# The last expert pairs of a decoder layer: where the combines of pairs 13 and 14 and the overflow branch stand

## Chip, cores and metric

One NeuronCore of a Trainium2 chip runs the whole layer in one launch. The metric is the device time of one execution in microseconds (us); lower is better.

## The reference, cut to what matters

The layer is a mixer of three branches (pooling, latent attention, attention into a memory), a residual add, then a mixture of experts with 32 experts of which each of the 512 tokens takes 2, another residual add and a last RMSNorm. Only the experts and the last norm are touched here. `D_MODEL` is 1024, `D_EXPERT` 256.

```
h2 = rms_norm(x, ffn_norm_g[l])
x = x + hierarchical_moe(h2, ...)
return rms_norm(x, final_norm_g)

def hierarchical_moe(h, ...):
    ...                                  # top group, top 2 experts of it, their weights
    def run_block(args):
        toks, e = args
        xb = x_pad[toks]
        a = jax.nn.silu(xb @ w_gate_e[e]) * (xb @ w_up_e[e])
        return a @ w_down_e[e]
    ...
    y = yb.reshape(R, D) * row_w[:, None].astype(yb.dtype)
    out = jax.ops.segment_sum(y, row_tok, num_segments=T + 1)[:T]
```

## The kernel before

The 32 experts are handled as 16 pairs, 64 token slots for each expert of a pair, so that a pair fills the 128 partitions. `W[e]` are the weights of an expert, in twelve pieces of 128x512; two pieces make one load of 512 KB. All loads go through one queue (SyncE, SP) into a ring of 36 places: tiles `e` of the pools W0 (tag `e0`, 6 places) and W1 (tag `e1`, 18 places), and tiles `r`, `wh`, `wl`, `m`, `ac` left from earlier stages. `used(n)` moves the ring on and lets further loads be written down.

The program is traced in the order in which the text calls the helpers (`tc.manual_schedule()`): each engine executes its own instructions in that order, and waits on semaphores where data come from another engine. For each pair `p` a list of short names gives the order:

- `U0` to `U7` (`up`, L1126): the gate and up products, step k of 8, accumulated in one bank `gu`. `U7` ends with silu on ScalarE (ACT, L1134) and a product on VectorE (DVE, L1135) into tile `a`.
- `t` (`turn`, L1137): TensorE transposes `a`, ACT copies it back (L1142).
- `D` (`down`, L1144, with `down_half`, L1161): the product with the down weights. Its two halves are scaled by the routing weight; ACT writes the rounded part (L1151), DVE the rest (L1152), into two tiles `y`. In step `p` these are called for pair `p-1`.
- `c` (`combine`, L1170): one of eight pieces of putting a pair's `y` onto its tokens. Two matmuls with the one-hot matrix `PT` put half a row tile in a bank (`xe` of two banks or `cb`, of which there is one), and DVE adds it to `ACC`, the residual stream in SBUF with tokens on partitions (L1176).
- `x0`, `x1` transpose the next pair's gathered tokens, `w` builds `PT`, `o`, `j`, `f` prepare a later pair (nothing, once there is none).

Pairs 0 to 8 add their output in DRAM by a scattering DMA. Pairs 9 to 14 are combined into `ACC`; the eight pieces wait in the list `todo` and are taken by the `c` of the order lists, four in a pair's own following step, four in the next. The last pair (15) isn't combined: TensorE gathers the `ACC` rows of its tokens into two banks (L1356, sixteen passes of 128x512 in the trace, four for each row tile), its down product is added there, and the rows get their own norm and go to the output by a scattering DMA (L1377). All 512 rows are normed and written before that (L1365, L1366); the scatter waits for these writes.

An expert with more than 64 tokens sets `flag`. `overflow()` then runs the pairs again for the rest. It stands in a branch (`tc.If`, L1295) that all engines read and jump over when `flag` is 0. In the profiled execution its body was jumped over. An engine that jumps adds to its own semaphores what the body would have added, after its own earlier work is done.

The lists of orders, and what is done ahead of the last pair:

```
SEQM = "o U0 c U1 j c U2 c t c U3 x0 D n U4 w c U5 c x1 c U6 f c U7".split()
SEQL = "t D U0 U1 U2 U3 U4 U5 U6 U7".split()
...
        if last:
            while todo:
                todo.pop(0)()
            ...
            with tc.If(nc.values_load(flag[0:1, 0:1], min_val=0, max_val=1) > 0):
```

Of the kernel before, what the change touches and what calls it, by code (L numbers as in the profile page):

```python
# [9 lines left out]
F32 = mybir.dt.float32  # L10
F32R = mybir.dt.float32r
BF16 = mybir.dt.bfloat16
I32 = mybir.dt.int32
AF = mybir.ActivationFunctionType
# [5 lines left out]
T = 512  # L20
D = 1024
# [20 lines left out]
def trunk_and_moe(ctx, tc, a, out):  # L42
    nc = tc.nc
    v, s, g, pe = nc.vector, nc.scalar, nc.gpsimd, nc.tensor
# [34 lines left out]
    def nm(b):  # L79
        n[0] += 1  # L80
        return f"{b}{n[0]}"
# [26 lines left out]
    def bank(p, tag, bufs, shape=(128, 512)):  # L108
        return p.tile(list(shape), F32, tag=tag, name=nm(tag), bufs=bufs)
# [9 lines left out]
    eps = cst.tile([128, 1], F32, name="eps")  # L119
# [99 lines left out]
    order = tc.manual_schedule()  # L219
# [104 lines left out]
    w = WS.use("w_in", 0)  # L324
# [172 lines left out]
    for h_ in range(XHEADS):  # L497
        fill()
        fill()
        w = WS.use("w_mk", h_)  # L500
# [3 lines left out]
        t = mt()  # L504
# [5 lines left out]
    for c in range(4):  # L510
        fill()
        fill()
        w = WS.use("w_mv", c)
# [19 lines left out]
    for h_ in range(XHEADS):  # L533
# [3 lines left out]
        for i in range(4):  # L537
            S = bank(PA, "s", 2)
# [18 lines left out]
        hs = slice(h_ * 128, (h_ + 1) * 128)  # L557
# [39 lines left out]
    b = swap(kr)  # L597
# [13 lines left out]
    scale = 192.0 ** -0.5  # L611
# [23 lines left out]
    for d in range(KD):  # L635
        w = WS.use("w_bpm", d)
# [15 lines left out]
    NP = NE // 2  # L652
# [147 lines left out]
    for h_ in range(HEADS):  # L800
        for op in SEQ:
# [22 lines left out]
            elif k == "V" and h_ % 2:  # L824
                p = (h_ + 1) // 2
# [44 lines left out]
    W1 = Scope("w1", side="right").p  # L870
# [55 lines left out]
    ACC = row_major()  # L926
# [65 lines left out]
    def ct2(dt=F32):  # L992
        return C2.tile([128, 1024], dt, tag="y", name=nm("y"), bufs=3)
# [58 lines left out]
    PC = Scope("pc", space=PSUM).p  # L1052
# [6 lines left out]
    extra = [False]  # L1059
# [4 lines left out]
    class Pair:  # L1064
# [78 lines left out]

        def down(self):  # L1144

            y = self.y = [ct2()] if self.scattered else [ct2(F32R), ct2(F32R)]
            for hf in range(2):
                hs = slice(hf * 512, (hf + 1) * 512)
                ps = self.down_half(hf)
                if not self.scattered:  # L1150
                    s.activation(y[0][:, hs], ps, AF.Copy, scale=self.wt)  # L1151
                    v.scalar_tensor_tensor(y[1][:, hs], ps, self.wt, y[0][:, hs].bitcast(F32), op0=OP.mult, op1=OP.subtract)  # L1152
                elif hf:
                    v.tensor_scalar(y[0][:, hs], ps, self.wt, None, op0=OP.mult)  # L1154
                else:
                    s.activation(y[0][:, hs], ps, AF.Copy, scale=self.wt)
            if self.scattered:
                g.indirect_dma_start(out=xo[:, :], out_offset=bass.IndirectOffsetOnAxis(ap=self.ix[:, :1], axis=0), in_=y[0], in_offset=None,  # L1158
                                     bounds_check=T - 1, oob_is_err=False, compute_op=OP.add)
# [113 lines left out]

    SEQ0 = "X0 b1 X1 b2 X2 U0 X3 U1 X4 U2 X5 U3 X6 U4 X7 U5 j0 o U6 j1 x0 U7 L x1 j2 j f".split()
    SEQM = "o U0 c U1 j c U2 c t c U3 x0 D n U4 w c U5 c x1 c U6 f c U7".split()
    SEQL = "t D U0 U1 U2 U3 U4 U5 U6 U7".split()
    todo = []
    fs = cst.tile([128, 5, 4], F32, name="fs")  # L1280

    def wide():
        return W0.tile([128, 2, T], F32, tag="e0", name=nm("e"), bufs=6).rearrange("p a b -> p (a b)")

    for p, q in enumerate(PP):
        q.wts = [W[2 * p], W[2 * p + 1]]
        last = p == NP - 1
        if p == NP - 2:
            gf = XG[0]
            g.dma_start(gf, a["final_g"].broadcast_to([128, D]))  # L1290
        if last:
            while todo:
                todo.pop(0)()
            order.__exit__(None, None, None)
            with tc.If(nc.values_load(flag[0:1, 0:1], min_val=0, max_val=1) > 0):  # L1295
                extra[0] = True
                overflow()
                extra[0] = False
            order = tc.manual_schedule()
            order.__enter__()  # L1300

            q.rw = fs[:, 0, 3:4]
            v.tensor_tensor(q.rw, q.rs, q.wt, op=OP.mult)
        for op in (SEQ0 if p == 0 else SEQL if last else SEQM):
            n_ = int(op[1]) if len(op) > 1 else p + 3
            if op[0] == "U":
                q.up(n_)
                if n_ % 2:
                    used(2)
            elif op == "c" and todo:  # L1310
                todo.pop(0)()
            elif op[0] == "X":
                q.pick_x(n_)
            elif op[0] == "b":
                PP[n_].fetch(PP[n_].by_slot(tokr, 2)[:, 0:1])
            elif op[0] == "x" and not last:
                PP[p + 1].turn_x(n_)
            elif op == "w" and SC <= p < NP - 1:
                q.where()
            elif op == "L":  # L1320
                PP[0].place(PP[0].it[:, 6:7])
                for i in range(RING - 4, RING):
                    load_piece(i)
            elif op == "n" and p == 1:
                tiles()
            elif op[0] in "ojf" and n_ < NP:
                if op[0] == "o":
                    PP[n_].onehot()
                if op[0] == "j":
                    PP[n_].info()  # L1330
                if op[0] == "f":
                    PP[n_].fetch(PP[n_].it[:, 6:7])
            elif op == "t":
                PP[p - 1].turn()
            elif op == "D":
                PP[p - 1].down()
                used(4)
                if p == SC:
                    ACC = row_major()
                    for t in range(4):  # L1340
                        g.dma_start(ACC[:, t].rearrange("p a b -> p (a b)"), xo[t * 128:(t + 1) * 128])
                if p > SC:
                    todo += [lambda i=i, q=PP[p - 1]: combine(i, q) for i in range(8)]

    junk, o = wide(), wide()
    hs = [slice(hf * 512, hf * 512 + 512) for hf in range(2)]
    s.activation(fs[:, 4, 0:1], q.a[:, 0:1], AF.Sqrt, scale=0.0)
    ys = [bank(PC, "y", 2) for hf in range(2)]
    for t in range(4):
        x = ACC[:, t].rearrange("p a b -> p (a b)")  # L1350
        todo.pop(0)()
        todo.pop(0)()
        if t == 1:
            q.turn()
        for hf in range(2):
            pe.matmul(ys[hf], lhsT=q.P[:, t].bitcast(F32), rhs=x[:, hs[hf]], start=t == 0, stop=False)  # L1356
        f = fs[:, t]
        s.activation(junk, x, AF.Square, accum_out=f[:, 0:1])
        s.activation(f[:, 1:2], f[:, 0:1], AF.Sqrt, bias=eps[:, 0:1], scale=1.0 / D)
    for hf in range(2):  # L1360
        q.down_half(hf, ys[hf])
    for t in range(4):
        x = ACC[:, t].rearrange("p a b -> p (a b)")
        v.reciprocal(fs[:, t, 2:3], fs[:, t, 1:2])  # L1364
        v.scalar_tensor_tensor(x, x, fs[:, t, 2:3], gf, op0=OP.mult, op1=OP.mult)  # L1365
        sync.dma_start(out[0, t * 128:(t + 1) * 128], x)  # L1366
    f = fs[:, 4]
# [103 lines left out]
```

## Time and profile before

| what | value |
| --- | --- |
| median of 3 runs | 805.36 us (804.89 to 809.42) |
| the profiled execution's own time | 807.81 us |
| its span in the profile | 806.0 us |
| TensorE (PE) busy | 779.0 us, 97% |
| DVE, ACT, GpSimd (POOL) busy | 365.8, 304.4, 276.8 us |
| mean granted TensorE clock | 0.991 of full speed |

The profiled execution is 1.8 us longer than its span, and 2.45 us longer than the median. A "busy" TensorE is not one at its peak, so its share says little; what counts near the end is which wait ends last. Times below are in us from the start of the span.

### The profile page before, as it was taken

The page shows a single profiled execution, that of the slowest core. Times are in us where ns is not written, and L with a number is a line of the kernel's source. Part 1 is how long each engine was busy: PE and PEld are TensorE (multiplying, and loading weights), DVE is VectorE, ACT ScalarE, POOL GpSimd, SP SyncE. Part 2 cuts the span into 40 slices and gives each one's busy share as a digit, 9 for nine tenths or more (in the row PEclk, how much of TensorE's full clock was granted, in tenths as well). Part 3 has the DMA queues.
Part 4 walks back from the last instruction along what each step waited for, and adds up shares of the span by engine and source line. Part 5 has one row for each costly group of instructions (what it writes and reads, how often), then busy time and mean ns, then how long its engine had stood idle before and what let it go on. Part 6 is the DMA issues. An engine that isn't in the chain of part 4 may idle for free. (4 is left out here: it accounts for less than half of the span.)

```text
span 806.0 us, 10157 instructions
## 1 busy us (share of the span) xinstructions
PE 779.0 (97%) x3741; PEld 524.1 (65%) x3743; DVE 365.8 (45%) x675; ACT 304.4 (38%) x626; POOL 276.8 (34%) x169
## 2 busy tenths in 40 slices
PE   7999999999999999999999999999999999999894
PEld 3778888888887888788888888754333333333331
DVE  5668693243455134677774532323121223454424
ACT  6254453343336444655553321213222222222232
POOL 3256677533332688422225644311121212000000
PEclk9999999999999999999999999999999999999988
DMA  6533333321121322111224489979999999999933
GB/s 223 179 105 105 105 105 136 125 105 71 62 92 38 98 95 92 46 47 56 79 87 176 147 313 340 372 257 354 394 370 397 391 374 392 405 354 408 405 125 120
DMA packets 53509, 164.17 MB, mean 204 GB/s; under 512 B 7906, under 2 KB 9058, under 8 KB 53456
## 3 DMA queue, kind: packets, MB, share of 16 engines
q1 hardware_dynamic: 46224, 149.14, 50.3%
q0 software_dynamic: 4640, 9.90, 3.8%
q10 hardware_dynamic: 2592, 4.46, 1.5%
q8 instruction: 30, 0.49, 0.2%
q14 instruction: 23, 0.19, 0.1%
HBM read 158.82 MB, written 11.53 MB: 211 GB/s over the span
## 5 line engine op out<-in xcount | busy, mean ns | idle before, releaser
L125 POOL TENSOR_TENSOR wl<-r,wh 128x1024 fp32r<-128x1024 f32 (+3 forms) x75 | 167.7, 2244 | 210.8 <-ACT wh L180 189.7
L180 ACT CAST wh<-r 128x1024 fp32r<-128x1024 f32 (+3 forms) x85 | 82.1, 972 | 32.0 <-PE mm L199 12.6
L1131 PE MATMUL gu<-e,u 128*64 128x512 f32 x336 | 88.8, 607 | 0.9 <-DMA e<-in_w_e 0.9
L198 PE MATMUL mm<-g,wh 128*128 128x512 f32 x180 | 71.9, 400 | 0.0
L199 PE MATMUL mm<-g,wh 128*128 128x512 f32 x180 | 70.2, 390 | 0.0
L1107 ACT ACTIVATE u<-xe,PR 128x128 f32<-128x128 f32 x120 | 34.2, 367 | 67.4 <-PE xe L1103 67.3
L471 PE MATMUL mm<-box,wh 128*128 128x512 f32 x144 | 56.8, 394 | 0.9 <-ACT wh L180 0.9
L472 PE MATMUL mm<-box,wh 128*128 128x512 f32 x144 | 56.3, 391 | 0.0
L201 PE MATMUL mm<-g,wl 128*128 128x512 f32 x180 | 52.7, 391 | 0.0
L1158 POOL DMA_INDIRECT xo<-y,ix x9 | 14.3, 1594 | 89.9 <-DVE ix L1082 79.7
L435 ACT ACTIVATE m<-s,st 128x256 f32<-128x256 f32 (+3 forms) x48 | 24.3, 508 | 54.4 <-DVE st L433 53.9
L1131 PEld LDWEIGHTS gu<-e,u 128*64 128x64 f32 x336 | 20.4, 135 | 33.0 <-issue 26.1
L1167 PE MATMUL y<-e,u 128*64 128x512 f32 x160 | 38.9, 600 | 0.4 <-DMA e<-in_w_e 0.4
L201 PEld LDWEIGHTS mm<-g,wl 128*128 128x128 f32 x180 | 33.8, 188 | 7.5 <-POOL wl L125 0.2
L198 PEld LDWEIGHTS mm<-g,wh 128*128 128x128 f32 x180 | 34.0, 189 | 6.5
L199 PEld LDWEIGHTS mm<-g,wh 128*128 128x128 f32 x180 | 33.9, 188 | 6.4
L476 PE MATMUL mm<-box,wl 128*128 128x512 f32 x144 | 36.6, 390 | 0.0
L198 PE MATMUL mm<-box,wh 128*128 128x512 f32 x78 | 31.7, 406 | 0.5 <-DVE g L283 0.5
L471 PEld LDWEIGHTS mm<-box,wh 128*128 128x128 f32 x144 | 27.1, 188 | 6.7 <-ACT wh L180 1.3
L1154 DVE TENSOR_SCALAR y<-y,it 128x512 f32<-128x512 f32 x9 | 6.8, 751 | 54.1 <-PE y L1167 54.1
L476 PEld LDWEIGHTS mm<-box,wl 128*128 128x128 f32 x144 | 27.0, 188 | 5.8
L472 PEld LDWEIGHTS mm<-box,wh 128*128 128x128 f32 x144 | 27.1, 188 | 5.3
(358 smaller groups left out, 1657.3 us busy)
## 6 DMA issues: line engine op xcount, KB each, us to landing
e<-in_w_e SPq DMA_DIRECT2D x124, 512.0 KB
r<-in_w_in SPq DMA_DIRECT2D x37, 512.0 KB
r<-in_w_e SPq DMA_DIRECT2D x15, 512.0 KB
wh<-in_w_e SPq DMA_DIRECT2D x15, 512.0 KB
wl<-in_w_e SPq DMA_DIRECT2D x15, 512.0 KB
m<-in_w_e SPq DMA_DIRECT2D x30, 256.0 KB
r<-in_w_bpm SPq DMA_DIRECT2D x8, 512.0 KB
r<-in_w_bl SPq DMA_DIRECT2D x8, 512.0 KB
```

Of the source, the lines that this page charges most:

```text
L125: eng.tensor_tensor(lo, x, hi.bitcast(F32), op=OP.subtract)
L180: s.copy(hi[:, :cols], r[:, :cols])
L198: pe.matmul(ps, lhsT=lh, rhs=rh, start=start and i == 0, stop=False)
L199: pe.matmul(ps, lhsT=lh, rhs=rl, start=False, stop=False)
L201: pe.matmul(ps, lhsT=ll, rhs=rh, start=False, stop=stop and i == m - 1)
L435: s.activation(P[:, :w], S[:, :w], AF.Exp, bias=st4[:, 0:1], accum_out=st4[:, 1:2])
L471: pe.matmul(ps, lhsT=lh, rhs=rh, start=k == 0, stop=False)
L472: pe.matmul(ps, lhsT=lh, rhs=rl, start=False, stop=False)
L476: pe.matmul(ps, lhsT=ll, rhs=rh, start=False, stop=k == KD - 1)
L1107: s.activation(x[:, j], ps[:, j], AF.Copy, scale=PR[:, k:k + 1])
L1131: pe.matmul(gu[r], lhsT=self.xe[k // 4][:, k % 4, r], rhs=self.wts[b][k], start=k == 0, stop=k == KD - 1)
L1167: pe.matmul(y[r], lhsT=self.aT[:, k, r], rhs=self.wts[b][8 + 2 * k + hf], start=k == 0 and not more, stop=k == 1)
```

## The change

The step of pair 14 gets an order list of its own (`SEQ14`), in which all eight combines of pair 13 stand behind `U4` to `U7` of pair 14. The list of the last pair (`SEQL`) now holds the combines of pair 14 in twos behind `U3` to `U7` of pair 15, the branch (`I`) behind `U3`, the squares of the rows (`s`), their square roots (`r3` for the first three rows, `r4` for the fourth, with the reciprocals of the first three), the gathers of the last pair (`S`) and its transposes (the second `t`). `y` of pair 13, and of the pairs that the overflow body runs, takes two places of the tag `e1` in the weight ring. The Sqrt of L1347 that stood ahead of the rows goes away.

```
@@ down
-            y = self.y = [ct2()] if self.scattered else [ct2(F32R), ct2(F32R)]
+            if extra[0] or self is PP[NP - 3]:
+                y = self.y = [W1.tile([128, 2, T], F32R, tag="e1", name=nm("y"), bufs=18).rearrange("p a b -> p (a b)") for _ in range(2)]
+            else:
+                y = self.y = [ct2()] if self.scattered else [ct2(F32R), ct2(F32R)]
@@ orders
-    SEQL = "t D U0 U1 U2 U3 U4 U5 U6 U7".split()
+    SEQ14 = "U0 c U1 c U2 c t c U3 x0 D U4 w U5 c c x1 c c U6 c c U7 c c".split()
+    SEQL = "t D U0 U1 U2 U3 I c c U4 s0 c c U5 s1 c c U6 s2 U7 r3 c c s3 r4 S0 S1 t S2 S3".split()
@@ ahead of the last pair
-            while todo:
-                todo.pop(0)()
-            order.__exit__(None, None, None)
-            with tc.If(nc.values_load(flag[0:1, 0:1], min_val=0, max_val=1) > 0):
...
+            junk, o = wide(), wide()
+            ys = []
@@ in the loop over the list
+            elif op == "I":
...
+                with tc.If(nc.values_load(flag[0:1, 0:1], min_val=0, max_val=1) > 0):
...
+            elif op[0] == "s":
+                s.activation(junk, tok_rows(n_), AF.Square, accum_out=fs[:, n_, 0:1])
+            elif op[0] == "r":
+                ts = slice(0, 3) if n_ == 3 else slice(3, 4)
+                s.activation(fs[:, ts, 1], fs[:, ts, 0], AF.Sqrt, bias=eps[:, 0:1], scale=1.0 / D)
+                if n_ == 4:
+                    v.reciprocal(fs[:, 0:3, 2], fs[:, 0:3, 1])
+            elif op[0] == "S":
...
+                for hf in range(2):
+                    pe.matmul(ys[hf], lhsT=q.P[:, n_].bitcast(F32), rhs=tok_rows(n_)[:, hs[hf]], start=n_ == 0, stop=False)
+            elif op == "t" and last and ys:
+                q.turn()
@@ behind the loop
-    s.activation(fs[:, 4, 0:1], q.a[:, 0:1], AF.Sqrt, scale=0.0)
-    for t in range(4):
-        todo.pop(0)()
-        todo.pop(0)()
-        if t == 1:
-            q.turn()
-        for hf in range(2):
-            pe.matmul(ys[hf], lhsT=q.P[:, t].bitcast(F32), rhs=x[:, hs[hf]], start=t == 0, stop=False)
...
```

TensorE, end of pair 14's step and start of the last one, before (`gu` is the gate and up bank of pair 14, `xe` and `cb` hold combines of pair 13, `at` the transposes of pair 14, `y_6655` its down product; the branch body is left out):

```order
L1131 MATMUL gu_6298<-e_6048,u_6277 64x512
L1174 MATMUL xe_6394<-y_6338,u_6260 128x512
L1174 MATMUL cb_6398<-y_6338,u_6260 128x512
L1174 MATMUL xe_6402<-y_6338,u_6260 128x512
L1174 MATMUL cb_6406<-y_6338,u_6260 128x512
L1295 TENSOR_LOAD flag
L1295 COMPARE_AND_BRANCH
...
L1140 MATMUL at_6649<-K,u_6391 128x128 x2
L1167 MATMUL y_6655<-r_6061,u_6391 64x512
```

The same place now:

```order
L1177 MATMUL cb_6383<-y_6338,u_6260 128x512
L1131 MATMUL gu_6298<-e_6046,u_6277 64x512
L1131 MATMUL gu_6298<-e_6048,u_6277 64x512
L1177 MATMUL xe_6389<-y_6338,u_6260 128x512
L1177 MATMUL cb_6393<-y_6338,u_6260 128x512
...
L1177 MATMUL xe_6402<-y_6338,u_6260 128x512
L1177 MATMUL cb_6406<-y_6338,u_6260 128x512
L1140 MATMUL at_6413<-K,u_6399 128x128 x2
L1170 MATMUL y_6419<-r_6061,u_6399 64x512
```

Two combines instead of four stand behind the last gate product of pair 14, and the branch no longer stands between them and the transposes.

TensorE in the last pair, from its last gate product on, before (`y_6692`, `y_6693` are the two banks of the gathered rows, `at_6714` the transposes of pair 15):

```order
L1131 MATMUL gu_6669<-m_6190,u_6374 64x512
L1174 MATMUL xe_6694<-y_6654,u_6357 128x512
L1174 MATMUL cb_6698<-y_6654,u_6357 128x512
L1356 MATMUL y_6693<-ACC_5743,P_6050 128x512
L1174 MATMUL xe_6706<-y_6654,u_6357 128x512
L1174 MATMUL cb_6710<-y_6654,u_6357 128x512
L1140 MATMUL at_6714<-K,u_6686 128x128 x2
L1356 MATMUL y_6692<-ACC_5743,P_6050 128x512
```

And now, from the branch on:

```order
L1335 UNCONDITIONAL_BRANCH
L1177 MATMUL xe_6680<-y_6418,u_6357 128x512
L1177 MATMUL cb_6684<-y_6418,u_6357 128x512
L1131 MATMUL gu_6433<-m_6147,u_6374 64x512
...
L1131 MATMUL gu_6433<-m_6190,u_6374 64x512
L1177 MATMUL xe_6719<-y_6418,u_6357 128x512
L1177 MATMUL cb_6723<-y_6418,u_6357 128x512
L1352 MATMUL y_6730<-ACC_5743,P_6050 128x512
L1352 MATMUL y_6731<-ACC_5743,P_6050 128x512
L1140 MATMUL at_6736<-K,u_6715 128x128 x2
```

Six of pair 14's eight combines moved from behind the last gate product to between the gate products, and the gathers follow each other.

ACT in the last pair, from the silu on, before:

```order
L1134 ACTIVATE u_6686<-gu_6669,it_6070 128x256
L1347 ACT_TABLE_LOAD
L1347 ACTIVATE fs<-u_6686 128x1
L1358 ACTIVATE e_6689,fs<-ACC_5743 128x1024
L1359 ACTIVATE fs<-fs,eps 128x1
L1142 COPY u_6686<-at_6714 128x256
```

The same place now:

```order
L1342 ACTIVATE e_6411,fs<-ACC_5743 128x1024
L1134 ACTIVATE u_6715<-gu_6433,it_6070 128x256
L1345 ACT_TABLE_LOAD
L1345 ACTIVATE fs<-fs,eps 128x3
L1342 ACTIVATE e_6411,fs<-ACC_5743 128x1024
L1345 ACTIVATE fs<-fs,eps 128x1
L1142 COPY u_6715<-at_6736 128x256
```

Three squares now stand ahead of the silu of pair 15; the table load, the fourth square and both roots stand between it and the copy of the transposes.

## Rows read from the trace of the kernel before

**Rows 1.** The page, part 2: mean busy tenths of the DMA engines in 40 slices

```profile
DMA  6533333321121322111224489979999999999933
```

**Rows 2.** Stretches: length, busy PE, PEld, DVE, ACT, POOL (count), clock, DMA share, GB/s

```profile
764.00:765.00 1.00, 0.08 (x1) 0.11 (x2) 0.23 (x1) 0.00 (x0) 0.00 (x0) 0.90 1.05 389
765.00:766.00 1.00, 0.58 (x2) 0.18 (x2) 0.00 (x0) 0.37 (x1) 0.00 (x0) 0.50 1.04 379
...
771.00:772.00 1.00, 1.00 (x6) 0.37 (x4) 0.32 (x1) 0.00 (x0) 0.00 (x0) 0.69 0.62 242
...
786.00:788.00 2.00, 1.69 (x6) 0.86 (x5) 1.26 (x2) 0.29 (x1) 0.00 (x0) 1.00 0.00 0
```

**Rows 3.** Timeline of pair 14's step: start, length, engine, line, out<-in, idle before

```profile
750.05 3.65 PE L1167 MATMUL y<-e,u 128*64 128x512 f32 x16
...
753.54 1.03 PE L1131 MATMUL gu<-e,u 128*64 128x512 f32 x4
...
758.74 0.30 PEld L1174 LDWEIGHTS cb<-y,u 128*128 128x128 f32 x2 [0.81 <-DVE ACC L1176]
...
759.40 0.20 PEld L1131 LDWEIGHTS gu<-e,u 128*64 128x64 f32 x4 [0.37 <-issue]
...
760.41 0.30 PEld L1174 LDWEIGHTS xe<-y,u 128*128 128x128 f32 x2 [0.81 <-issue]
...
760.75 0.42 PEld L1174 LDWEIGHTS cb<-y,u 128*128 128x128 f32 x2
...
761.04 0.48 DVE L1135 SCALAR_TENSOR_TENSOR u<-gu,it,u 128x256 f32<-128x256 f32 x1 [0.84 <-ACT u L1134]
...
762.77 0.73 PE L1174 MATMUL cb<-y,u 128*128 128x512 f32 x2 [0.70 <-DVE ACC L1176]
...
764.92 0.66 PE L1140 MATMUL at<-K,u 128*128 128x128 f32 x2 [1.42 <-DVEq L1295]
```

**Rows 4.** The branch at L1295 by queue: count, duration ns, first and last start

```profile
L1295 SPq EVENT_SEMAPHORE  x9: 17/17/17, 772.3 to 773.9; - x9
...
L1295 DVEq EVENT_SEMAPHORE  x2: 21/21/21, 764.8 to 764.9; - x2
...
L1295 PEldq TENSOR_LOAD <-flag x1: 488/488/488, 762.8 to 762.8; - x1
L1295 PEldq COMPARE_BRANCH  x1: 445/445/445, 763.4 to 763.4; - x1
```

**Rows 5.** The chain of waits in order of time, last pair

```profile
766.04 6.41 PE y L1167 x16
772.45 6.92 PE gu L1131 x32
...
781.03 1.98 PE y L1356 x4
783.02 0.48 PE xe L1174 x2
...
783.52 0.70 DVE ACC L1176
...
796.92 2.65 DMA out_dram<-ACC
```

**Rows 6.** Timeline of the end of the last pair

```profile
792.62 3.65 PE L1167 MATMUL y<-e,u 128*64 128x512 f32 x16
...
796.32 0.60 ACT L1369 ACTIVATE e<-y 128x512 f32<-128x512 f32 x1 [1.00 <-PE y L1167]
...
798.25 0.72 ACT L1375 ACTIVATE e<-e,fs 128x512 f32<-128x512 f32 x1 [0.31 <-DVE fs L1374]
...
800.44 1.02 POOL L1377 DMA_INDIRECT out_dram<-e,ix  x1 [59.74 <-DMA out_dram<-ACC]
```

**Rows 7.** Timeline of SP: issues of the last weight loads

```profile
755.82 6.76 SPq L686 DMA_DIRECT2D m<-in_w_e  x6
763.53 2.94 SPq L686 DMA_DIRECT2D e<-in_w_e  x4
```

More of the change, by code (lines that the diff above doesn't have):

```diff
@@ L1277, in trunk_and_moe @@
     SEQM = "o U0 c U1 j c U2 c t c U3 x0 D n U4 w c U5 c x1 c U6 f c U7".split()
-    SEQL = "t D U0 U1 U2 U3 U4 U5 U6 U7".split()
+    SEQ14 = "U0 c U1 c U2 c t c U3 x0 D U4 w U5 c c x1 c c U6 c c U7 c c".split()
+    SEQL = "t D U0 U1 U2 U3 I c c U4 s0 c c U5 s1 c c U6 s2 U7 r3 c c s3 r4 S0 S1 t S2 S3".split()
     todo = []
+    hs = [slice(hf * 512, hf * 512 + 512) for hf in range(2)]
+    tok_rows = lambda t: ACC[:, t].rearrange("p a b -> p (a b)")
     fs = cst.tile([128, 5, 4], F32, name="fs")
@@ L1291, in trunk_and_moe @@
         if last:
-            while todo:
-                todo.pop(0)()
-            order.__exit__(None, None, None)
-            with tc.If(nc.values_load(flag[0:1, 0:1], min_val=0, max_val=1) > 0):
[L1296 to L1300, printed above, removed]
             q.rw = fs[:, 0, 3:4]
             v.tensor_tensor(q.rw, q.rs, q.wt, op=OP.mult)
-        for op in (SEQ0 if p == 0 else SEQL if last else SEQM):
+            junk, o = wide(), wide()
+            ys = []
+        for op in (SEQ0 if p == 0 else SEQL if last else SEQ14 if p == NP - 2 else SEQM):
             n_ = int(op[1]) if len(op) > 1 else p + 3
@@ L1332, in trunk_and_moe @@
                     PP[n_].fetch(PP[n_].it[:, 6:7])
+            elif op == "I":
+                order.__exit__(None, None, None)
+                with tc.If(nc.values_load(flag[0:1, 0:1], min_val=0, max_val=1) > 0):
+                    extra[0] = True
+                    overflow()
+                    extra[0] = False
+                order = tc.manual_schedule()
+                order.__enter__()
+            elif op[0] == "s":
[6 more added lines that the diff above has]
+            elif op[0] == "S":
+                if n_ == 0:
+                    ys += [bank(PC, "y", 2) for hf in range(2)]
+                for hf in range(2):
+                    pe.matmul(ys[hf], lhsT=q.P[:, n_].bitcast(F32), rhs=tok_rows(n_)[:, hs[hf]], start=n_ == 0, stop=False)
+            elif op == "t" and last and ys:
+                q.turn()
             elif op == "t":
@@ L1343, in trunk_and_moe @@
                     todo += [lambda i=i, q=PP[p - 1]: combine(i, q) for i in range(8)]
-    junk, o = wide(), wide()
-    hs = [slice(hf * 512, hf * 512 + 512) for hf in range(2)]
-    s.activation(fs[:, 4, 0:1], q.a[:, 0:1], AF.Sqrt, scale=0.0)
-    ys = [bank(PC, "y", 2) for hf in range(2)]
-    for t in range(4):
-        x = ACC[:, t].rearrange("p a b -> p (a b)")
-        todo.pop(0)()
-        todo.pop(0)()
-        if t == 1:
-            q.turn()
-        for hf in range(2):
-            pe.matmul(ys[hf], lhsT=q.P[:, t].bitcast(F32), rhs=x[:, hs[hf]], start=t == 0, stop=False)
-        f = fs[:, t]
-        s.activation(junk, x, AF.Square, accum_out=f[:, 0:1])
-        s.activation(f[:, 1:2], f[:, 0:1], AF.Sqrt, bias=eps[:, 0:1], scale=1.0 / D)
     for hf in range(2):
@@ L1362, in trunk_and_moe @@
     for t in range(4):
-        x = ACC[:, t].rearrange("p a b -> p (a b)")
-        v.reciprocal(fs[:, t, 2:3], fs[:, t, 1:2])
+        x = tok_rows(t)
+        if t == 3:
+            v.reciprocal(fs[:, t, 2:3], fs[:, t, 1:2])
         v.scalar_tensor_tensor(x, x, fs[:, t, 2:3], gf, op0=OP.mult, op1=OP.mult)
```

## The prediction, as put on record

> **What bounds the kernel now.** I read the page's forty slices first. The DMA engines are at nine tenths or more from slice 27 to 38 [rows 1]: the expert stage waits for weights, until the last of them have landed. The rows of stretches show where that ends: DMA share 1.04 at 765, 0.62 at 771 [rows 2]. The SP queue gives the last load away at about 766.5 [rows 7], and its nine semaphore steps of the branch, each behind the loads of one semaphore, end at 773.9 [rows 4]. So the last weights are there 32 us before the span's end, and behind that only TensorE's order decides. The change touches nothing before pair 14's second half, so only what follows 753.5 can move.
>
> The chain of waits from there [rows 5] is TensorE nearly throughout: pair 14's down product, 32 passes of gate products of pair 15, then gathers and combines in turn with DVE, then DVE's norms, the row DMA and the scatter. Three things on it are not work. Four leftover combines of pair 13 wait for DVE's adds, since `cb` is one bank (0.70 idle at 762.77), and the branch keeps TensorE from 763.50 to 764.92 [rows 3], because DVE is through it only at 764.9 [rows 4]. In this thin stretch the granted clock falls from 2.4 to 1.2 GHz (0.90 in 764 to 765, 0.50 after), and it is back only in the stretch 771 to 772 [rows 2], so the down product of pair 14 takes 6.41 us [rows 5] where that of pair 13 took 3.65 [rows 3]. And from 781 on each gather of 1.98 waits for the combine and the add ahead of it, 0.48 + 0.70 [rows 5].
>
> **The change, part by part,** from the first gate pass behind pair 13's down product, 753.54 [rows 3].
>
> *Pair 14's step.* Before, 6.87 us pass until the first combine behind `U7` is loaded (760.41). Two of the four later combines now stand ahead of that point, each beside another combine. Two in a row follow at 0.34 (760.41, 760.75), and DVE must first have emptied the bank, so I take 0.45; the bounds are 0.34 and the 0.77 that each cost in the drain at the end (four in 3.09, 760.41 to 763.50) [rows 3]. That gives 753.54 + 6.87 + 0.9 = 761.3. The last two combines then cover the silu and the product into `a`, which ends 1.11 behind that load (761.52 against 760.41 [rows 3]). So the transposes start at 762.4. Transposes and copy took 1.12 up to the down product (764.92 to 766.04 [rows 3, 5]) with the clock at half; 0.85 is my estimate at full clock. The down product starts at 763.25 instead of 766.04: **2.8 gained**. Its weights are not late: they were issued ahead of the `m` and `e` loads of rows 7.
>
> *Its down product.* Without the drain and the branch the longest gap ahead of it is the copy's 0.4, so I take the full clock: 3.65 instead of 6.41 [rows 3, 5], **2.75 gained**, end at 766.9 instead of 772.45.
>
> *Gate products of pair 15.* 6.92 as before [rows 5]. Their weights are `r`, `wh`, `wl` and `m`. The last `m` is issued at 762.6 [rows 7]; the last load of all took at most 7.4 from issue to the end of SP's semaphores (766.5 to 773.9), so `m` is there by 770, and `U6`, its user, comes at 775. Inserted are six combines in three twos: 0.34 and then 0.66 to the next gate product (758.74 to 759.40), and 0.15 more at each change from gate product to combine (759.40 to 760.41 is 1.01, the passes are 0.86 of it) [rows 3], 1.15 a two, **3.45 lost**. DVE's two adds of 0.70 lie beside the gate products of about 0.86 and the changes.
>
> *The branch* is moved, not added. TensorE's queue read the flag in 0.49 and branched in 0.445, 1.25 with its semaphores (762.8 to 764.05) [rows 4], but it began at 762.8, when the last combine's passes had started and had 0.7 still to run [rows 3]. That leaves about **0.5 lost**; it is 1.25 if nothing runs ahead, and 0.2 if the reading hides wholly behind `U0` to `U3`. DVE and ACT, for which the next combine waits, have ended their parts of `y` some 5.2 behind the start of the down product by my estimate (768.4), and are through the branch before TensorE comes at 770.3. SP's part ends at 773.9, but nobody waits for it: before, the down product started at 766.04 behind the same branch. The Trainium skill, "PSUM — Partial Sum Buffer", section "Engine vs sequencer instructions", says that the sequencer waits only until earlier instructions are handed to the engine, not until they end. The trace agrees (flag read at 762.8, passes until 763.50); by that rule alone the branch would cost the 0.2, by the row 0.5.
>
> So the gate products end at 766.9 + 6.92 + 3.45 + 0.5 = 777.75 instead of 779.37: 1.6 gained so far.
>
> *From there to pair 15's down product.* Before, 13.25 (779.37 to 792.62). Now two combines, 0.9 until the first gather's pass; four gathers without a wait, 1.72 each (1.98 less the 0.26 by which one pass runs on into the next), 6.9; the transposes 0.4, with the silu hidden behind two gathers. Sum 8.2, down product at 785.95: **6.7 gained in all**. ACT's table load, fourth square and roots, some 3.5 us behind the silu, end at about 782 and lie under the gathers; the copy that the down product needs is not late. The squares on ACT cost nothing, they lie under the gate products. If this cover were gone, the copy would be late by as much as ACT's chain is longer.
>
> *The end.* Before, the scatter was let go by the row DMA, 796.92 + 2.65 = 799.57, 6.95 behind the start of the down product. Now DVE is free while the gathers run, norms the first three rows under them, and the fourth ends 1.3 behind the last gather, so the row DMA lands at about 790. What ends last is the other branch: the second half's square started 3.70 behind the down product (796.32 against 792.62) and its scaling ended at 6.35 (798.97) [rows 6], of which DVE's late rows made some 0.4. I take 6.1: scatter let go at 792.05 instead of 799.57, **7.5 gained**. What follows it, to the end of the span, is unchanged.
>
> *`y` of pair 13 in two places of the weight ring* costs nothing if these are the oldest places: SP's list of loads ends with `e` on tag `e0`, no load follows on `e1`, and the places taken held weights used before this product. If ACT had to wait for the newest loads instead, it would be by up to the 7.4 above, of which the combines would pass on some 5.
>
> **The sum** is -7.5 us: 807.81 becomes 800.3 for an execution like the profiled one, and 805.36 becomes **797.8** for the median. That is 0.93%; about 1% (8.05 us) is what a measurement of this kernel tells from no change, so the forecast lies just on the near side of it.
>
> **Rivals.**
> 1. *The clock falls all the same*, at the branch or at the transposes of pair 14, and comes back after 6.8 us as before (764.9 to 771.7 [rows 2]). Then half of that is lost: +3.4, **801.2**. For: the branch still stops TensorE at full DMA load. Against: from 762 to 766 TensorE stood still again and again (0.70, 1.42 [rows 3]), now there is one gap of 0.5; and between 786 and 788, with 1.69 of 2 us busy, the clock stayed at 1.00 [rows 2].
> 2. *Each combine pays the round trip to DVE.* With one `cb`, the second of a two waits for the add of the second of the two before. If that is as in the drain, eight combines that now stand in twos cost 0.77 instead of some 0.45: +2.6, **800.4**. Against: between two twos there lies about 1 us of gate products.
> 3. *The branch stalls.* TensorE's compare-and-branch took 445 ns [rows 4]. If code behind the jump comes late and no reading is hidden, the gap is the 1.42 of before or a little more instead of 0.5: +1, **798.8**. The Trainium skill, "Runtime: NRT & Kernel Launch", section "Instruction fetch mechanics", says that a taken branch out of the fetched window waits for a DMA fetch; by that rule the stall is paid at either place, and this trace doesn't show a fetch apart from the 445 ns.
> 4. *It gives more:* branch hidden, combines at 0.34: another 1.3, **796.5**.
> 5. *The change doesn't do what it says:* the place in the ring makes ACT wait, the combines come no earlier, +5, **802.8**.
> 6. *Slower than before:* the clock falls at the branch and doesn't come back while combines and gate products alternate. Each 2 us at half clock lose 1. The gain of 7.5 is used up when it stays low for 15 us; TensorE's work from the branch to the end of the last down product is 19 us at full clock, so low throughout costs up to 19 and gives **813**. For: such a mixed stretch has more gaps than the dense product in which the clock came back. Against: rows 2, 786 to 788.
>
> **How the numbers follow.** Forecast 0.58 (own range 796.6 to 799.4), rival 1 0.13, rival 2 0.10, rival 3 0.06, rival 4 0.08, rival 5 0.03, rival 6 0.02. The range 795.5 to 802.0 takes in all but rivals 5 and 6 and the ends of the others, some 1 in 6. Faster by over 1% means below 797.3: rival 4 and about half of the forecast, 0.37. Slower by over 1%: rival 6, 0.02. Within 1%: 0.61.
>
> **What would show it.** The down product of pair 14 at about 763 with some 3.65 us; granted clock 1.00 from 760 to 790; one gap of about half a us at the branch near 770; gate products ending near 777.7; sixteen gather passes in under 7.5 us; the last down product at 786; and the scatter let go by ACT or DVE, not by the row DMA. A clock of 0.50 behind the branch would show rival 1 or 6, gaps before the second combine of a two rival 2, a late first `y` of pair 13 rival 5. I am wrong if the clock fell in the profiled run of before but not in most, since 2.75 of the gain is that fall.

## The result, and the profile after

The changed kernel took **801.79 us** (median of 13 runs, 799.83 to 804.63) where the kernel before took 807.92 (13 runs, 804.89 to 811.6) beside it: ratio 0.9928 [0.9913, 0.9942], 5.8 us less (the medians by themselves lie 6.1 apart). In a second comparison it was 801.56 (6 runs) against 806.85 (22 runs), ratio 0.9943 [0.9928, 0.9958], 4.6 us less (medians 5.3 apart); one run of each kernel there, 1286.88 and 2695.33 us, was in a slow state and is no part of the ratio. Gains in us below are those of the ratios. The intervals are some 0.15% wide to either side, so a gain of 0.7% is told from no change, though it is under the 1% that I had set for that. The forecast was 797.8: right in sign, and 4.0 too low. Of these, 2.6 lie in the level (the three runs of before that I started from had a median of 805.36, the thirteen of the comparison 807.92), 1.4 in the gain (6.1 between the medians, forecast 7.5).

The profiled execution of the changed kernel took 801.2 us, its span is 799.4. The DMA line of the page is that of [rows 1] in its kind: weights are awaited up to slice 38.

```profile
DMA  6532333322221322211115379988999999999963
```

Two executions never start their last stage at the same time: pair 13's down product starts at 750.95 here and at 750.05 in [rows 3], and the change touches nothing ahead of that. So I read both traces from this product on.

Stretches of the changed kernel, with the columns of [rows 2]. Where the clock had fallen to 0.50 before, it is 1.00 throughout:

```profile
764.00:765.00 1.00, 0.76 (x4) 0.34 (x6) 0.55 (x2) 0.19 (x1) 0.00 (x0) 1.00 1.04 391
765.00:766.00 1.00, 1.00 (x6) 0.29 (x4) 0.00 (x0) 0.00 (x0) 0.00 (x0) 1.00 1.05 391
...
771.00:772.00 1.00, 0.54 (x3) 0.24 (x2) 0.00 (x0) 0.00 (x0) 0.00 (x0) 1.00 0.95 385
...
786.00:788.00 2.00, 2.00 (x8) 0.58 (x8) 1.64 (x3) 0.00 (x0) 0.00 (x0) 1.00 0.70 281
```

Timeline of TensorE around pair 14's step of the changed kernel, with the columns of [rows 3]:

```profile
762.18 0.72 PE L1177 MATMUL xe<-y,u 128*128 128x512 f32 x2
762.75 0.63 PE L1177 MATMUL cb<-y,u 128*128 128x512 f32 x2
763.35 0.44 PE L1140 MATMUL at<-K,u 128*128 128x128 f32 x2
764.25 0.64 PE L1170 MATMUL y<-r,u 128*64 128x512 f32 x1 [0.46 <-ACT u L1142]
```

The idle 0.70 and 1.42 of [rows 3] are gone: combines run up to the transposes, and only ACT's copy leaves 0.46 idle ahead of the down product of pair 14, which starts 13.30 behind that of pair 13 (15.99 in [rows 3, 5]).

The branch, now at L1335, by queue, with the columns of [rows 4]:

```profile
L1335 SPq EVENT_SEMAPHORE  x9: 17/17/17, 773.3 to 775.6; - x9
...
L1335 PEldq EVENT_SEMAPHORE  x2: 51/51/51, 771.4 to 771.5; - x2
L1335 PEldq TENSOR_LOAD <-flag x1: 489/489/489, 766.9 to 766.9; - x1
L1335 PEldq COMPARE_BRANCH  x1: 352/352/352, 767.5 to 767.5; - x1
```

TensorE's queue reads the flag at 766.9 and jumps at 767.5, while its passes up to `U3` still run to 771.3. Only the two semaphore steps at 771.4 and 771.5 stand in the open. SP's part ends at 775.6, and no row waits for it. TensorE is idle for 0.46 ahead of the first combine (771.33 to 771.79); the chain of waits starts behind the two steps, with 0.19 in which nothing was waited for that the profile shows:

```profile
771.60 0.19 issue
771.79 0.70 PE xe L1177 x2
772.49 0.47 PE cb L1177 x2
772.96 1.01 PE gu L1131 x4
773.97 0.66 PE xe L1177 x2
774.62 0.47 PE cb L1177 x2
775.09 1.01 PE gu L1131 x4
776.10 0.66 PE xe L1177 x2
776.75 0.47 PE cb L1177 x2
777.22 1.87 PE gu L1131 x8
779.09 0.66 PE xe L1177 x2
779.75 0.46 PE cb L1177 x2
780.22 3.43 PE y L1352 x8
783.65 0.22 PE at L1140 x2
783.87 3.44 PE y L1352 x8
787.30 3.61 PE y L1170 x16
```

Behind this 0.19 every link is TensorE at work. The combines wait for no add and the gathers for no combine, where [rows 5] had 0.48 and 0.70 between any two gathers. Each two of combines (one in `xe`, one in `cb`) takes 1.12 to 1.17.

The end of the changed kernel, timeline, to be held against [rows 6]:

```profile
792.45 0.72 ACT L1383 ACTIVATE e<-e,fs 128x512 f32<-128x512 f32 x1 [0.50 <-DVE fs L1382]
...
793.79 1.02 POOL L1385 DMA_INDIRECT out_dram<-e,ix  x1 [52.19 <-ACT e L1383]
```

The scatter is now let go by the scaling of its rows and no longer by the row DMA: the timeline names ACT's half of the scaling, the chain of waits DVE's, which ends at 792.95.

From pair 13's down product to the end this execution takes 48.45 us, that of before 55.95: **7.5 less, which is the forecast** (48.4 to the end; its small misses cancel, as shown below). So the two profiles bear out the sum, and the two comparisons give 5.8 and 4.6 of it. What is to be explained is this difference.

### The profile page after: what moved, and what is told of

Its sections match the earlier page's. It is cut to its first block, busy times and chain, and to the rows that moved or that the text cites. A ratio compares the mean times of both kernels' runs of the same rounds, so it can differ in the third digit from the quotient of the medians.

```text
span 799.4 us, 10154 instructions
## 1 busy us (share of the span) xinstructions
PE 775.8 (97%) x3743; PEld 523.8 (66%) x3743; DVE 366.3 (46%) x673; ACT 303.6 (38%) x623; POOL 277.1 (35%) x169
## 5 line engine op out<-in xcount | busy, mean ns | idle before, releaser
L198 PE MATMUL mm<-g,wh 128*128 128x512 f32 x180 | 71.9, 400 | 0.0
L435 ACT ACTIVATE m<-s,st 128x256 f32<-128x256 f32 (+3 forms) x48 | 24.4, 509 | 54.5 <-DVE st L433 54.0
L198 PEld LDWEIGHTS mm<-g,wh 128*128 128x128 f32 x180 | 34.0, 189 | 6.4
L198 PE MATMUL mm<-box,wh 128*128 128x512 f32 x78 | 31.7, 406 | 0.9 <-DVE g L283 0.9
```

Of the source, the lines that this page charges most:

```text
L198: pe.matmul(ps, lhsT=lh, rhs=rh, start=start and i == 0, stop=False)
L435: s.activation(P[:, :w], S[:, :w], AF.Exp, bias=st4[:, 0:1], accum_out=st4[:, 1:2])
```

## The experiments

The first theory, T1: the fall of the clock, 2.75 of the 7.5, is not in every execution of the kernel before, or not whole. The rival, T2: it is in all of them, and the stretch ahead of pair 13's down product, which differs by execution, hid a part of the gain in the comparison. A third, T3: some step of the change gives less than its profile shows.

### One part of the change alone

*Only the last pair's new order.* Combines of pair 14 between the gate products of pair 15, gathers without waits; pair 14's step and the branch as before. Against the changed kernel:

```
-            if extra[0] or self is PP[NP - 3]:
+            if False:
...
-    SEQL = "t D U0 U1 U2 U3 I c c U4 s0 ...
+    SEQL = "t D U0 U1 U2 U3 c c U4 s0 ...
...
         if last:
+            while todo:
+                todo.pop(0)()
+            ...                              (the branch, as before)
...
-        for op in (SEQ0 if p == 0 else SEQL if last else SEQ14 if p == NP - 2 else SEQM):
+        for op in (SEQ0 if p == 0 else SEQL if last else SEQM):
```

> The last pair's new order alone: pair 14's combines in twos between the gate products, squares and gathers as in the change; pair 13's combines, its y, and the branch as before. My theory: down product of pair 14 at 766.04 and slow as before, gate products 3.45 longer, then 5.05 shorter to the last down product, 0.8 at the end: 2.4 us faster than before. Rival, combines in twos cost DVE's round trip: 0.5 or less faster. Rival, the tail is all of the gain: 5 to 6 faster.

Measured: 805.23 against 807.93, ratio 0.9965 [0.9951, 0.9979], 2.8 less. In its profile the clock fell as in the one of before (pair 14's down product 6.33), and from pair 13's down product to the end it took 53.32, 2.6 less than 55.95. Profile and comparison agree: this part gives what it shows.

*Only pair 14's new order and the place of `y`.* The drain of `todo`, the branch and the last pair stand as before. Against the kernel before:

```
+            if self is PP[NP - 3]:
+                y = self.y = [W1.tile([128, 2, T], F32R, tag="e1", ...
...
+    SEQ14 = "U0 c U1 c U2 c t c U3 x0 D U4 w U5 c c x1 c c U6 c c U7 c c".split()
...
-        for op in (SEQ0 if p == 0 else SEQL if last else SEQM):
+        for op in (SEQ0 if p == 0 else SEQL if last else SEQ14 if p == NP - 2 else SEQM):
```

> Pair 14's new order and the place of pair 13's y alone; the branch ahead of the last pair and the last pair's order as before. My theory: DVE's last add ends at 764.4 as before, since the same eight adds end the step, so the transposes stand behind the branch at about 765.1 and nothing is gained but where the clock stays up: 0 if it falls (0.50 in the records behind 765), 2.5 faster if the denser end of the step holds it. Rival, the leftover combines themselves were the cost: 2.8 or more faster, with the clock as before.

Measured: 805.94 against 807.93, ratio 0.9978 [0.9962, 0.9993], 1.8 less. In the profile TensorE waits 1.42 at the branch and the clock falls, but for a shorter time: the down product takes 5.35, not 6.41, and 53.65 pass to the end. The time that the clock stays low is thus no constant. The expectation that the step itself gains nothing failed: from pair 13's to pair 14's down product it takes 14.71 (750.75 to 765.46), where the profiles of the kernel before have 15.74 to 15.99.

*The branch ahead of the last pair*, all else as changed. Against the changed kernel:

```
-    SEQL = "t D U0 U1 U2 U3 I c c U4 s0 ...
+    SEQL = "I t D U0 U1 U2 U3 c c U4 s0 ...
```

> The changed kernel, but with the branch where it was, ahead of pair 14's transposes. My theory: DVE's last add ends at 764.5 and DVE is through the branch some 0.7 later, so the transposes start near 765.2 instead of 763.35 (+1.9), the 0.5 behind U3 goes away, and the thin stretch lets the clock fall (+2.75): 4.1 us slower than the change, so 2 to 3.5 us faster than before. If the clock has no share in the gain: 1.4 us slower than the change, with the clock at 1.00 or with its fall costing nothing in the time. Rival, the branch's place is worth nothing: same as the change.

Measured: 803.99 against 807.93, ratio 0.9956 [0.9941, 0.9971]: 3.6 less than before, some 2 more than the changed kernel. Its timeline and its stretches:

```profile
765.07 0.41 PE L1140 MATMUL at<-K,u 128*128 128x128 f32 x2 [1.42 <-DVEq L1335]
```

```profile
766.00:768.00 2.00, 2.00 (x6) 0.61 (x8) 0.00 (x0) 0.00 (x0) 0.00 (x0) 0.58 1.01 363
768.00:770.00 2.00, 2.00 (x8) 0.62 (x6) 0.00 (x0) 0.63 (x1) 0.00 (x0) 0.57 0.98 368
```

Without the wait of 0.70 for a leftover combine, the 1.42 at the branch still comes with a fall of the clock, and the down product takes 5.35. From pair 13's down product to the end are 51.07, 2.6 more than in the changed kernel, where I expected 4.1: 1.4 of stop (14.71 against 13.30 between the two down products) and 1.7 of clock, less the 0.5 at the branch behind `U3` that goes away. So of what pair 14's step gains, the branch's place gives 1.4 and the combines' order 1.0 to 1.3 (15.74 to 15.99 before, 14.71 here).

### Work instead of the pause

Six passes that nobody reads, put between the leftover combines and the branch of the kernel before.

```
             while todo:
                 todo.pop(0)()
+            keep = bank(PC, "at", 1)
+            for i in range(6):
+                pe.matmul(keep, lhsT=KB[:, 0:128], rhs=KB, start=True, stop=True)
```

> The kernel before, with six dummy matmuls of 128x512 (bfloat16, into the free bank at) behind the leftover combines, ahead of the branch; nothing reads them. It measures the clock's fall by itself. My theory: TensorE stays busy to about 764.8, the clock stays at 1.00, the down product of pair 14 takes 3.65 instead of 6.41; the transposes start 0 to 0.4 later: 2.3 to 2.75 us faster than before if the clock falls in every execution of before, some 1.3 if it falls in half of them. Rival, the clock's fall is not on the path (weights set the end): same as before. If the fill doesn't hold the clock: 0 to 0.4 slower.

Measured: 805.68 against 807.93, ratio 0.9973 [0.9958, 0.9988], 2.2 less. The passes run 1.47 us in the pause, 0.45 stays idle, the clock holds 1.00, and the down product takes 3.65. From pair 13's down product to that of pair 14 it still takes 16.08 us, so the pause as such is not shortened; 53.29 pass to the end. What comes back is the clock alone. If it held in all six runs, of which one was profiled, this measures what its fall costs the kernel before on average: 2.2, 1.0 to 3.4 by the interval.

### Without the branch

```
             order.__exit__(None, None, None)
-            with tc.If(nc.values_load(flag[0:1, 0:1], min_val=0, max_val=1) > 0):
-                extra[0] = True
-                overflow()
-                extra[0] = False
             order = tc.manual_schedule()
```

> The kernel before with the overflow branch taken out (it leaves out the overflow of experts with more than 64 tokens). TensorE's stop of 1.42 us at the branch goes. Theory A, that this stop is what lets the clock fall: pair 14's down product takes 3.65 instead of 6.41 us, in all 1.4 + 2.75 = 4.2 us off, about 803.8 against 807.9. Theory B, that the waits of the leftover combines for DVE let it fall as well: the down product still takes more than 5 us in the profile and 1.4 us come off, 806.5.

Measured: 807.08 against 806.85, ratio 1.0013 [1.0, 1.0027]. Neither theory: nothing came off at all. Yet in the profile the clock holds, and from pair 13's down product to the end 52.01 us pass. The loss lies some 300 us and more ahead of the edit. The first passes of L895 started 353.87 behind the first ones of L198 with `wh<-u` weights (116.15 to 470.02); in the kernel before these are 351.25 (116.91 to 468.16). The passes themselves take longer. By source line, with count, and shortest, median and longest ns, first without the branch, then with it (the changed kernel, run again):

```profile
L198 PE MATMUL mm<-g,wh x180: 392/396/483, 270.3 to 459.9; 128*128 128x512 f32 x180
```

```profile
L198 PE MATMUL mm<-g,wh x180: 387/389/487, 271.5 to 458.8; 128*128 128x512 f32 x180
```

The overflow's small tiles live in the pool of constants. Without them the pools behind it begin 288 bytes lower in SBUF (six tiles, each taken in steps of 32 bytes). The same happened to the changed kernel without its branch (`I` taken out of `SEQL`):

> The changed kernel with the branch taken out (it leaves out the overflow of experts with more than 64 tokens). In the changed kernel's profile TensorE loses 0.46 us at the branch. Theory, that TensorE's sequencer reads and branches ahead of its matmuls and only this rest is left: 0.3 to 0.6 us off the changed kernel, not to be told from it. Rival, that the code behind the jump or the queues' semaphores cost more than the gap shows: 1.4 us or more off.

Measured: 803.09 against 806.85, ratio 0.9963 [0.995, 0.9977], 1.5 more than the changed kernel beside it (801.56), with 353.94 us for that same stretch. So both were made again with an unused tile that puts the addresses back:

```
+    pad = cst.tile([128, 69], F32, name="pad")
+    g.memset(pad[:, 0:1], 0.0)
```

> The kernel before without the branch (it leaves out the overflow of experts with more than 64 tokens), with an unused tile of 276 bytes in the pool of constants, so that every tile of the trunk lies at the address that it has in the kernel before; without it they lie 288 bytes lower, and the passes of the trunk ran some 7 ns longer. Theory, that the addresses made those passes longer: the stretch from 117 to 468 us takes 351.3 again instead of 353.9, and from pair 13's down product on it takes 52.0 instead of the 55.95 of before, so the median is 3.5 to 4 us under before. Rival, that the place of the code in memory made them longer: the stretch stays at 353.9 and the median at before.

> The changed kernel without the branch (it leaves out the overflow of experts with more than 64 tokens), with the same unused tile. Theory of the addresses: the stretch from 117 to 468 us takes 351.3, and the median is 0.4 to 0.6 us under the changed kernel, since its gap at the branch is 0.46 us. Rival, the place of the code: 353.9 and 1.5 us slower than the changed kernel, as without the tile.

Measured: the kernel before without the branch 805.6 against 807.77, ratio 0.9974 [0.9958, 0.9991], 2.1 less; the changed one without it 801.76, ratio 0.9921 [0.9897, 0.9946] to before, the same as the changed kernel in its two comparisons (801.79 and 801.56). The stretch took 351.33 in both, and the passes are back:

```profile
L198 PE MATMUL mm<-g,wh x180: 387/389/487, 270.3 to 457.6; 128*128 128x512 f32 x180
```

The theory of the addresses holds, the place of the code is out. For the branch: in the kernel before its removal was worth 2.1 and not the 3.5 to 4 that I expected from one profile. It isn't the branch alone, for TensorE's order changed with it: the last combine of pair 13 now stands behind the transposes (762.85) and the first two passes of pair 14's down product, whose others follow from 765.36:

```profile
763.70 1.07 PE L1167 MATMUL y<-r,u 128*64 128x512 f32 x2 [0.46 <-ACT u L1142]
764.70 0.73 PE L1174 MATMUL cb<-y,u 128*128 128x512 f32 x2
```

So 12.70 pass from pair 13's to pair 14's down product, 25.46 to that of pair 15 and 14.14 to the end, 52.30 in all; the three profiles of before, below, have 54.5 on average, and the difference, 2.2, is near the 2.1 of the comparison. What the stop at the branch costs by itself in the kernel before, these runs don't separate. In the changed kernel the branch costs nothing that can be measured; from the last pair's view it shows 0.5 (22.49 us from pair 14's to pair 15's down product, 22.98 with the branch).

### The kernel before, again

This is the test of T1 against T2: further profiles of the unchanged kernel.

> The kernel before itself, for another profile. If the clock falls at the branch in nearly every execution, pair 14's down product takes over 5 us again and 55 to 56 us pass from pair 13's down product to the end; if it falls in only a part of them, some of these profiles show 3.65 and 53.3.

> The kernel before itself, for a third profile, as the one ahead of it: over 5 us and 55 to 56 us, or 3.65 and 53.3.

Stretches of the first of them, 804.7 us of span:

```profile
764.00:766.00 2.00, 0.53 (x4) 0.32 (x6) 0.32 (x1) 0.37 (x1) 0.00 (x0) 0.94 1.07 386
766.00:768.00 2.00, 2.00 (x6) 0.64 (x8) 0.00 (x0) 0.00 (x0) 0.00 (x0) 0.50 1.04 387
768.00:770.00 2.00, 2.00 (x8) 0.51 (x6) 0.00 (x0) 0.44 (x1) 0.00 (x0) 0.71 1.02 384
```

and its chain of waits at pair 14's down product:

```profile
765.88 5.27 PE y L1167 x16
```

Stretches of the second, 804.1 us of span:

```profile
764.00:766.00 2.00, 0.61 (x2) 0.18 (x2) 1.11 (x2) 0.00 (x0) 0.00 (x0) 1.00 1.04 390
766.00:768.00 2.00, 1.51 (x8) 0.69 (x10) 0.00 (x0) 0.37 (x1) 0.00 (x0) 1.00 1.07 386
768.00:770.00 2.00, 2.00 (x12) 0.61 (x10) 0.31 (x1) 0.69 (x1) 0.00 (x0) 1.00 1.03 388
```

its timeline, and its chain:

```profile
763.88 0.73 PE L1174 MATMUL cb<-y,u 128*128 128x512 f32 x2 [0.70 <-DVE ACC L1176]
766.03 0.41 PE L1140 MATMUL at<-K,u 128*128 128x128 f32 x2 [1.42 <-DVEq L1295]
```

```profile
766.90 3.65 PE y L1167 x16
```

The waits are the same 0.70 and 1.42 in all three profiles of the kernel before, and pair 14's down product takes 6.41, 5.27 and 3.65. The clock fell wholly, for a shorter time, and not at all. The second and third profile are from the same chip, so this is not a difference between chips. T1 is shown. The changed kernel, profiled again beside the second comparison, repeats itself:

> The changed kernel itself once more, for the comparison within this call. If the 5.8 us of the first comparison are the mean gain, the median is 801.5 to 802.5 beside 807.9 of before; if the 7.5 us that the two profiles show from pair 13's down product on are the gain of a typical execution and the first comparison was low by chance, it is 800 to 801.

It took the 801.56 named above: the first of the two cases, though beside a before of 806.85. The stretches of all five, from start to start of the down products of pairs 13, 14 and 15, and on to the end of the span, in us:

| execution | 13 to 14 | 14 to 15 | 15 to end | sum | 13 starts at |
|---|---|---|---|---|---|
| before, as in the rows | 15.99 | 26.58 | 13.38 | 55.95 | 750.05 |
| before, second profile | 15.74 | 25.45 | 13.37 | 54.56 | 750.14 |
| before, third profile | 15.74 | 23.85 | 13.35 | 52.94 | 751.16 |
| forecast of the change | 13.2 | 22.7 | 12.5 | 48.4 | |
| changed | 13.30 | 22.98 | 12.17 | 48.45 | 750.95 |
| changed, again | 13.29 | 22.99 | 12.10 | 48.38 | 750.92 |

The three of before have a mean of 54.5, so the change is worth 6.1 on their average, against 5.8 [4.7, 7.0] and 4.6 [3.4, 5.8] us of the two comparisons (the intervals are those of the ratios, taken of 807.9 and 806.9). The whole spans of these executions, with what lies ahead of pair 13's down product, are 804.9 and 799.35 on average, 5.6 apart.

### A shorter gather for the last pair

With all of the chain on TensorE, the longest thing left to shorten is the sixteen fp32 gather passes, 6.9 us.

```
+    SEQL = "t D U0 U1 U2 U3 I c c U4 h0 s0 c c U5 h1 s1 c c U6 h2 U7 r0 c h3 c h4 G0 G1 t S2 S3 S6 S7 s2 s3 r2 q0 q1 q2".split()
...
+    elif op[0] == "h":                       (row tile r_, columns c_)
+        hi, lo = parts[r_]
+        s.copy(hi[:, c_], tok_rows(r_)[:, c_])
+        (g if n_ < 3 else v).tensor_tensor(lo[:, c_], tok_rows(r_)[:, c_], hi[:, c_].bitcast(F32), op=OP.subtract)
...
-                    pe.matmul(ys[hf], lhsT=q.P[:, n_].bitcast(F32), rhs=tok_rows(n_)[:, hs[hf]], start=n_ == 0, stop=False)
+                        pe.matmul(ys[hf], lhsT=q.P[:, n_ % 4], rhs=parts[n_ % 4][j][:, hs[hf]], start=op == "G0" and j == 0, stop=False)
```

The list also puts the norms of the first three rows (`q0` to `q2`) and their second roots (`r2`) behind the gathers.

> The changed kernel with the last pair's sixteen fp32 gather passes replaced: each row tile of ACC is split into a rounded part (ACT) and its rest (GpSimd for three row tiles, DVE for the last), and both parts are gathered in single passes, as the combines do. Theory, that TensorE's gathers bound the end of the changed kernel: 16 passes of 0.427 us become 16 of 0.214, 3.4 us less, of which the last row tile's split and DVE's norms give back some 0.5 to 1: 2.5 to 3 us faster than the changed kernel, about 799. Rival, that DVE's norms and the row DMA then end last: 1 us faster. Rival, that GpSimd's subtractions come late or slow DVE: no gain.

Measured: 802.06 against 806.85, ratio 0.9947 [0.9929, 0.9964], the same as the changed kernel beside it (0.9943). The gather passes did shrink (eight in 2.00 us instead of 3.59), but they now wait. From its timeline, TensorE, ACT, GpSimd and DVE:

```profile
786.68 1.95 PE L1368 MATMUL y<-y,P 128*128 128x512 f32 x5 [2.03 <-ACT y L1361]
```

```profile
776.59 1.05 ACT L1361 CAST y<-ACC 128x1024 fp32r<-128x1024 f32 x1 [6.65 <-SPq L1343]
```

```profile
777.72 7.10 POOL L1362 TENSOR_TENSOR y<-ACC,y 128x1024 fp32r<-128x1024 f32 x3 [34.83 <-ACT y L1361]
```

```profile
784.13 1.25 DVE L1362 TENSOR_TENSOR y<-ACC,y 128x512 fp32r<-128x512 f32 x1 [1.04 <-ACT y L1361]
```

ACT's first copy is let go by SP's way through the branch; I take it that this is because its tile is a place of the weight ring, and the first to be taken behind the branch. The three subtractions on GpSimd follow at 2.37 each, and a subtraction on DVE stands ahead of the last add, so the last row tile is split only at 787. Behind the idle 2.03 the clock fell as well, and the last down product took 4.73 instead of 3.65:

```profile
788.00:790.00 2.00, 2.00 (x6) 0.53 (x6) 2.00 (x3) 1.43 (x3) 0.00 (x0) 0.50 0.17 68
```

What ended last was DVE's norms and the row DMA:

```profile
792.69 2.74 DMA out_dram<-ACC
```

So the second and the third case of its expectation are at work together, and the time is that of the third. Nothing here beats the changed kernel; whether the split gains with tiles from elsewhere was not tried.

## Why the prediction was right in its mechanism and wrong in its size

*Pair 14's step: right.* I forecast 13.2 from down product to down product; it was 13.30 and 13.29. The pairs of combines at the end cost what I took.

*Its down product, "2.75 gained": this is the step that failed.* I made the sum against one execution, and put the 2.75 into the forecast for the median as if every execution of before had the same fall. What it rests on measured 2.76, 1.62 and 0 in three profiles (6.41, 5.27 and 3.65 against 3.65), 1.5 on average, with identical waits ahead of it. The dummy passes gave 2.2 [1.0, 3.4] for the same term. The prediction named this condition as what would make it wrong; it should have given it a chance and a price among the rivals. Half of the fall would have made the gain 6.1.

*The level: the larger part of the miss in the number.* Of the 4.0 us between 797.8 and 801.79, 2.6 are no step of the change. I took the 7.5, read in an execution of 807.81, off the median of three runs, 805.36; the four comparisons put the kernel before at 806.85 to 807.93. From 807.9, the mean gain of 6.1 gives 801.8.

*In the changed kernel the clock held, as forecast.* From 760 to 790 it is at 1.00 in both of its profiles, and rivals 1 and 6 did not come.

*Gate products and combines: a little too cheap.* From the first two to the end of the gate products 7.30 us pass (771.79 to 779.09). Half of the 32 gate passes lie in it, 3.46 of the 6.92, so three twos with their changes cost 3.84, forecast 3.45: a two takes 1.12 to 1.17 where I had 0.34 + 0.66. No wait for DVE stands between its two combines, so that is not the round trip of rival 2.

*Branch: right by luck.* It cost 0.46 to 0.49, forecast 0.5, and the 1.42 of rival 3 did not come. But TensorE's queue was 4 us ahead of its passes at the flag, so reading and jumping were hidden altogether. For this case the prediction had 0.2; its 0.5 stood for a reading that begins 0.7 ahead of the end of the passes. What stays are the two semaphore steps and the time to the next pass; what fills that time no row shows. The page's two queues of kind instruction have packets near both branches (one at 764 to 765 before, two at 771 to 772 now), and no row tells whether TensorE waited for them.

*From the gate products' end to pair 15's down product: right.* 8.14 (779.09 to 787.23), forecast 8.2; sixteen gather passes in 6.9 us, as said.

*The end: right.* 12.17 and 12.10 from that product to the end of the span, forecast 12.5, and ACT or DVE lets the scatter go. That the profile's 48.45 meets the 48.4 of the sum so closely is luck in part: 0.1 too little for pair 14's step and 0.3 for the gate products stand against 0.3 too much here.

*The place of `y` of pair 13: cost nothing, as forecast* (rival 5); the combines that read it start with no wait.

*Two slips that change nothing:* the DMA engines stand at seven tenths in slice 27 and at nine only from slice 28 [rows 1], and rival 6 with the clock low throughout is 797.8 + 19 = 816.8, not 813.

*What can be told:* I took 1% as the bound of a measurement. Thirteen runs of each kernel tell 0.15%, and the 0.7% that came out lies in the case "within 1%", to which I gave 0.61, but it is a gain and not a tie.

*What stays open:* three profiles don't give the average of the fall well, and the second comparison is 1.5 under their mean. T2 has a share that I can't separate: the start of pair 13's down product lies between 750.05 and 751.16 in the five executions of the table, for reasons ahead of the change. Why the clock fell in two executions and not in the third, after the same pauses, no run here shows. It can fall in other stages too: in the profile of the filled kernel it is at 0.50 from 531 to 537, and pair 13's down product starts at 754.01 there, some 3 later than in the table; such falls are a likely part of the spread from run to run.

## What to carry to other kernels

A fall of the clock seen in one profile is a chance and not a constant: profile the kernel two or three times before a term of a sum rests on it, and reckon with the mean. A branch that nothing takes was cheap here (0.5 us) where TensorE had queued work and DVE was through it first, and it cost 1.4 us and sometimes the clock where TensorE had drained and waited for DVE to come through. Before an edit is read from its total time, compare a stretch that it can't touch: removing code removed small tiles, shifted every pool and cost 2.6 us in another stage. Such a removal can also change the order of what is left, so the order is to be read again before the time is put down to what was removed.

## What the runs showed of the hardware that I had not expected

- **Addresses of tiles.** With the pools 288 bytes lower, passes of L198 from `g` and `wh` took 396 instead of 389 ns (median of 180), and 351.3 us of dense TensorE work became 353.9. With the tiles moved back by an unused tile, both numbers returned. In the same profiles the 78 passes of L198 from `box` and `wh` kept their median of 389 ns, which points to `g` and not to `wh`; which address does it was not tried.
- **TensorE's queue runs ahead.** It read the flag 4.4 us before the end of the passes written ahead of the branch (766.9, passes to 771.3). Reading a flag took 489 ns there and comparing and jumping 352 (445 in [rows 4]); the jump took 45 on ACT's and SP's queues and 72 on DVE's.
